# A down projection in seven products: ten pairs of K tiles in place of nine, set closer together, and later transpositions

## The chip, the cores and the metric

One program runs on one core of a Trainium2 chip. The metric is the device time of an execution in microseconds. Engines are named as the profile does: PE (TensorE), DVE (VectorE), ACT (ScalarE), POOL (GpSimd), SP (SyncE, which only issues DMAs here).

## The reference

One layer of a decoder trunk on 256 tokens of width 2048, all in fp32: two token mixers and their output projection, a gated feed-forward part, and a gated addition of a per-layer embedding.

```python
x = x + jnp.concatenate([ha, hb], axis=-1) @ w_out[i]
h = rms_norm(x, ffn_norm_g[i])
u = h @ w_up[i]                                   # 2048 -> 2 * 5632
a, g = jnp.split(u, 2, axis=-1)
a = causal_dwconv(a, conv_w[i], conv_b[i])        # width 3
x = x + (jax.nn.gelu(a, approximate=False) * g) @ w_down[i]      # 5632 -> 2048
gate = jax.nn.sigmoid(rms_norm(x, ple_norm_g[i]) @ w_ple_gate[i])
x = x + gate * (p[i].astype(x.dtype) @ w_ple_proj[i])
```

The change is in the product with `w_down` and in what follows it directly.

## The kernel before

Each fp32 product is made of three products in the narrower format fp32r: a matrix is split into `hi`, its rounding, and `lo`, the rest, and `hi*hi`, `hi*lo` and `lo*hi` are added in PSUM. Weights come as raw fp32 blocks of 128 rows by 1024 columns (512 KB) on SP's queue; ACT makes `hi` by a cast (line 836), DVE makes `lo` by a subtraction (line 837). Activations are split once, when they are made.

The work is a list of units (`Unit`), each with its loads (`load`), its split (`split`) and its matmuls (`fn`). `run_units` walks the list: ahead of a unit's matmuls it emits loads as long as raw buffers are free (3, and 2 more, `RAW2`, from the first unit of the down projection on) and splits up to 4 units ahead (7 in the down projection, `PARTS + PARTS2`). The framework's scheduler then sets the order of the instructions on each engine and its DMA queue; that order is fixed before the run, and each engine follows it, waiting on semaphores.

The down projection (`down`) runs in two halves of 1024 output columns, one after the other. Each half runs over 44 K tiles of 128, as 22 pairs, and in four PSUM banks it gathers the result by two halves of the tokens (`t`) and two of the columns (`n`); more banks hold what several of them share.

- An ordinary pair is two units of `eight`: for each K tile four products of 3 matmuls (lines 882 to 884) of 512 columns, so 24 matmuls a pair. A unit takes one raw block, one cast and one subtraction, each 1024 wide.
- A pair in `SEVEN` is taken as a 2x2 block matrix and multiplied by a scheme of seven block products in place of eight: 21 matmuls in four units. The first (`split1`) loads the kept left sums on SP's queue (line 913) and splits 512 columns of the first raw block, the second (`split2`) splits the second block; then `split3` and `split4` each make two sums of weights in place, by two DVE subtractions of 512 columns (lines 930 and 931, 940 and 941), and split the 1024 columns that come of it. A pair holds its two raw blocks until the third and the fourth split are done.

The left sums of these pairs are made in the up projection: `up_g` calls `left_sums` for each pair in `SEVEN` (lines 760 to 771), which makes four sums on DVE, splits them and writes them to DRAM through POOL's queue. In the down projection they are read back into two buffers in turn, so a load must wait until PE has done the seven-pair before last.

At the last pair in `SEVEN`, `sums_done` adds the shared banks to `xs` on DVE; after the last pair, `add_rest` adds the other four (line 995). The last stage, the gate, needs `xs` transposed (`transposes`, `transpose_x`, line 149): the first eight tiles hang on units of the second half, the last eight on the first units of the gate's first group, `g_`, whose eight units each use two tiles.

Of the kernel before, what the change touches and what calls it, by code (L numbers as in the profile page):

```python
# [33 lines left out]
RAW, PARTS = 3, 4  # L34
RAW2, PARTS2 = 2, 3

SEVEN = (2, 4, 6, 8, 10, 12, 14, 16, 18)
AHEAD_DMA, AHEAD_SPLIT = 3, 3
PAD = 16

# [5 lines left out]
def layer_kernel(  # L46
# [21 lines left out]
    def f32(ap):  # L68
        return ap.bitcast(F32)
# [63 lines left out]
    def split_T(dst, src, scale=None):  # L133

        hi, lo = dst[..., 0:256], dst[..., 256:512]
        if scale is None:
            act.copy(hi, src)
            dve.tensor_sub(lo, src, f32(hi))
        else:
            act.activation(hi, src, AF.Copy, scale=scale)  # L140
            dve.scalar_tensor_tensor(out=lo, in0=src, scalar=scale, in1=f32(hi),  # L141
                                     op0=ALU.mult, op1=ALU.subtract)

    def transpose_x(dst, k0, g):

        for k in (k0, k0 + 1):
            bk = bank("aux", f"xT{k}")
            for t in range(NT):
                pe.transpose(bk[:, t * P : (t + 1) * P], xs[:, t, k * P : (k + 1) * P], ident)
            split_T(dst[:, k, :], bk[:, 0:256], scale=g[:, k : k + 1])  # L150
# [91 lines left out]
    def token_group(w, korder, actT, c0, n, finish, tag="mm", prep=None, load=None):  # L242

        st = {}
        blocks = []
        kb = min(BLK // n, 2 * len(korder))
        starts = [(k0, kb) for k0 in korder[:: kb // 2]]
        if load is not None:
            starts = [(0, 1), (1, 1)] + starts[1:]
        for bi, (k0, kb) in enumerate(starts):  # L250
            def fn(hi, lo, bi=bi, k0=k0):
                if bi == 0:
                    st["b"] = [bank(tag, f"tg{t}") for t in range(NT)]
                for t in range(NT):
                    o = st["b"][t][:, :n]
                    for i in range(hi.shape[1]):
                        a = actT()[:, k0 + i, :]
                        ah, al = a[:, t * P : (t + 1) * P], a[:, 256 + t * P : 256 + (t + 1) * P]
                        first = bi == 0 and i == 0
                        last = bi == len(starts) - 1 and i == hi.shape[1] - 1  # L260
                        pe.matmul(o, ah, hi[:, i, :], start=first, stop=False)  # L261
                        pe.matmul(o, ah, lo[:, i, :], start=False, stop=False)  # L262
                        pe.matmul(o, al, hi[:, i, :], start=False, stop=last)  # L263
                    if bi == len(starts) - 1:
                        finish(t, st["b"][t])
            pair = k0 % 2 == 0
            blocks.append((wsrc(w, k0, kb, c0, n), fn, pair and prep and (lambda k0=k0: prep(k0)) or None,
                           pair and load and (lambda k0=k0: load(k0)) or None))
        return blocks
# [445 lines left out]
    with tc.tile_pool(name="ffn", bufs=1) as fp, tc.tile_pool(name="kept", bufs=1, space=bass.MemoryType.DRAM) as kp:  # L715
# [12 lines left out]

        sums = kp.tile([len(SEVEN), P, 1024], F32, name="sums")

# [29 lines left out]
        def left_sums(p_, u):  # L760

            (a11, a21), (a12, a22) = ((u[:, j, 0:P], u[:, j, P:S]) for j in range(2))
            f = sm.tile([P, 512], F32, tag="junk", name="Sf").rearrange("p (i c) -> p i c", i=4)
            dve.tensor_add(f[:, 0], a21, a22)
            dve.tensor_sub(f[:, 1], f[:, 0], a11)
            dve.tensor_sub(f[:, 2], a11, a21)
            dve.tensor_sub(f[:, 3], a12, f[:, 1])
            t = fp.tile([P, 4, 256], F32R, tag="pT", name="Sp")
            act.copy(t[:, :, 0:P], f)
            dve.tensor_sub(t[:, :, P:256], f, f32(t[:, :, 0:P]))  # L770
            pool.dma_start(out=sums[SEVEN.index(p_)], in_=f32(t).rearrange("p i c -> p (i c)"))

        def up_g(q):
            st = {}

            def f(jj, b):
# [5 lines left out]
                if j == 1:  # L782
                    dve.tensor_mul(u, u, gl.pop((q, pair)))
                    dst = uA[:, k : k + 2, :] if k < KD else uB[:, k - KD : k - KD + 2, :]
                    split_T(dst, u)
                    if k // 2 in SEVEN:
                        left_sums(k // 2, u)
# [51 lines left out]
        def units(blocks):  # L839
            return [Unit([b[0]], b[1], shift=b[4] if len(b) > 4 else 0) for b in blocks]  # L840
# [22 lines left out]
        def down(c0, X_tag, P_tag, sums_done, done, at):  # L863
# [4 lines left out]
            pairs = range(KF // 2)  # L868
            plain = [p_ for p_ in pairs if p_ not in SEVEN]
            total = {"P1": len(SEVEN), "P5": len(SEVEN), "P6": len(SEVEN), "P7": len(SEVEN)}  # L870
            for t in range(NT):
                for n in range(2):
                    total[t, n] = 2 * len(plain) + (len(SEVEN) if (t, n) != (1, 1) else 0)

# [90 lines left out]
        def get_x3T():  # L965
            if "t" not in x3T:
                x3T["t"] = new_aT("x3T")
            return x3T["t"]
# [30 lines left out]
        def transposes(*ks):  # L999
            return lambda *_: [transpose_x(get_x3T(), k0, g_ple) for k0 in ks]  # L1000
# [25 lines left out]
        def gate_done(c0, n, last):  # L1026
            def f(t, b):
                if "r" not in r3:
                    r3["r"] = rstd_of(ssq3, "ple")
                sg = fp.tile([P, 2, S], F32, tag="gl", name="sg", bufs=3).rearrange("p a b -> p (a b)")[:, :n]  # L1030
                w = n // 2 if last and t == NT - 1 else n
                for c in range(0, n, w):
                    sc = sg[:, c : c + w]
                    act.activation(sc, b[:, c : c + w], AF.Sigmoid, scale=r3["r"][:, t : t + 1])
                    dve.tensor_mul(sc, sc, pj[t][:, c : c + w])
                    dve.tensor_add(sc, sc, xs[:, t, c0 + c : c0 + c + w])
                    q = act if last and t == NT - 1 and c else nc.sync
                    q.dma_start(out=out[0, t * P : (t + 1) * P, c0 + c : c0 + c + w], in_=sc)
            return f

        def with_after(u, hook):
            fn = u.fn
            u.fn = lambda hi, lo: (fn(hi, lo), hook())
# [10 lines left out]
        for c0, n in ((0, 512), (512, 512), (1024, 512), (1536, 256), (1792, 256)):  # L1054
            g_ = units(token_group(w_ple_gate, all_k, get_x3T, c0, n, gate_done(c0, n, c0 == 1792)))
            p_ = units(token_group(w_ple_proj, [0], lambda: pT["t"], c0, n, proj_done, tag="aux"))
            if c0 == 0:
                for i in range(4):
                    with_after(g_[i], transposes(8 + 2 * i))
            at = len(g_) // 2  # L1060
            us += g_[:at] + p_ + g_[at:]
        run_units(us, first_late)
# [30 lines left out]
```

## Time and profile before

| | us |
|---|---|
| runs, median of 3 | 1280.36 (1279.6 to 1280.57) |
| the profiled execution | 1280.42 |
| its span, first to last instruction | 1278.7 |
| PE busy in it | 1269.0 |
| DVE busy in it | 851.3 |
| ACT busy in it | 681.8 |

The granted TensorE clock was 1.00 in the mean. The profile is of one execution. Its busy times are sums over instructions, taken over the whole kernel; the down projection runs from 938.5 to about 1169 us and has shares of its own, which the views by stretch show. A wait is put down to the work that ended last before it.

### The profile page before, as it was taken

What the parts mean: (1) busy time and instruction counts of PE and PEld (TensorE: products, weight loads), DVE (VectorE), ACT (ScalarE), POOL (GpSimd) and SP (SyncE); (2) the same over time, 40 slices, a digit from 0 to 9 for tenths busy, and PEclk for the clock granted to TensorE, in tenths of its full rate; (3) what the DMA queues carried; (4) which work ended last, traced back from release to release, by engine and by line L of the source; (5) the groups of instructions that cost most, each with busy time, mean ns of one, the idle gap of its engine ahead of it and who ended that gap; (6) DMA issues with size and microseconds to landing.
All of it is one profiled execution on the core that took longest, in us unless ns stands there. A gap on an engine that the chain in (4) does not pass through costs nothing.

```text
span 1278.7 us, 18356 instructions
## 1 busy us (share of the span) xinstructions
PE 1269.0 (99%) x7006; PEld 1112.0 (87%) x7006; DVE 851.3 (67%) x1173; ACT 681.8 (53%) x1011; POOL 23.6 (2%) x43
## 2 busy tenths in 40 slices
PE   9999999999999999999999999999999999999998
PEld 7899999988888888888888888888887788887888
DVE  6455566554555566776767676676778899898553
ACT  7655554434544455555555455555545556556442
POOL 2000000000000000000000000000000000000000
PEclk9999999999999999999999999999999999999999
DMA  8676755546555656676666766666767776777661
GB/s 249 172 188 186 209 172 147 153 134 180 170 187 180 188 180 197 185 210 202 198 198 204 209 191 207 206 207 190 213 220 245 259 281 221 253 243 238 198 192 46
DMA packets 124474, 252.87 MB, mean 198 GB/s; under 512 B 8377, under 2 KB 28193, under 8 KB 124385
## 3 DMA queue, kind: packets, MB, share of 16 engines
q1 hardware_dynamic: 122400, 246.51, 63.8%
q0 software_dynamic: 1600, 5.01, 1.1%
q8 instruction: 55, 0.90, 0.3%
q14 instruction: 34, 0.28, 0.1%
q10 hardware_dynamic: 385, 0.16, 0.0%
HBM read 244.84 MB, written 6.82 MB: 197 GB/s over the span
## 4 chain that ended last, share of the span: by engine, by line
PE 92%; DMA 3%; DVE 3%; ACT 1%; issue 0%; SPq 0%; DVEq 0%; ACTq 0%
PE wg L311 25%; PE wg L312 13%; PE tg L263 11%; PE tg L262 10%; PE tg L261 10%; DMA raw<-in_w_down_dram 2%; PE fg L287 2%; PE fg L289 2%; PE fg L288 2%; DMA raw<-in_w_in_dram 1%; DVE w L837 1%; PE dnP L884 1%; PE dnP L883 1%; PE dnP L882 1%; PE dn(0, 0)_9875 L884 1%; PE dn(0, 0)_9875 L882 1%
## 5 line engine op out<-in xcount | busy, mean ns | idle before, releaser
L311 PE MATMUL wg<-x2T,hi 128*128 128x512 f32 x1408 | 488.3, 392 | 0.0
L837 DVE TENSOR_TENSOR lo<-raw,hi 128x1024 fp32r<-128x1024 f32 (+1 forms) x268 | 320.3, 1203 | 177.2 <-ACT hi L836 176.3
L836 ACT CAST hi<-raw 128x1024 fp32r<-128x1024 f32 (+1 forms) x268 | 275.5, 1035 | 280.1 <-PE wg L311 177.4
L312 PE MATMUL wg<-x2T,lo 128*128 128x256 f32 x1408 | 393.5, 280 | 0.0
L311 PEld LDWEIGHTS wg<-x2T,hi 128*128 128x128 f32 x1408 | 264.1, 188 | 56.4
L233 DVE TENSOR_TENSOR lo<-raw,hi 128x1024 fp32r<-128x1024 f32 (+2 forms) x161 | 179.5, 1116 | 159.5 <-ACT hi L231 158.9
L312 PEld LDWEIGHTS wg<-x2T,lo 128*128 128x128 f32 x1408 | 267.3, 190 | 0.1
L231 ACT CAST hi<-raw 128x1024 fp32r<-128x1024 f32 (+2 forms) x161 | 154.6, 960 | 174.0 <-PE tg L263 100.4
L262 PE MATMUL tg<-lo,hT 128*128 128x512 f32 (+1 forms) x384 | 136.6, 356 | 0.5 <-DVE lo L233 0.5
L261 PE MATMUL tg<-hi,hT 128*128 128x512 f32 (+1 forms) x384 | 136.1, 358 | 0.0
L263 PE MATMUL tg<-hi,hT 128*128 128x512 f32 (+1 forms) x384 | 135.7, 355 | 0.0
L836 ACT CAST w<-raw 128x1024 fp32r<-128x1024 f32 x69 | 67.4, 988 | 57.9 <-DMA raw<-in_w_down_dram 22.1
L837 DVE TENSOR_TENSOR w<-raw,w 128x1024 fp32r<-128x1024 f32 x69 | 78.2, 1143 | 24.8 <-ACT w L836 24.4
L262 PEld LDWEIGHTS tg<-lo,hT 128*128 128x128 f32 x384 | 72.2, 188 | 8.2 <-DVE lo L233 1.0
L263 PEld LDWEIGHTS tg<-hi,hT 128*128 128x128 f32 x384 | 72.0, 188 | 7.7 <-DVE hT L141 0.3
L261 PEld LDWEIGHTS tg<-hi,hT 128*128 128x128 f32 x384 | 71.8, 188 | 7.1
L287 PE MATMUL fg<-hT,hi 128*128 128x256 f32 x256 | 74.3, 290 | 0.0
L289 PE MATMUL fg<-hT,lo 128*128 128x256 f32 x256 | 72.8, 284 | 0.0
L288 PE MATMUL fg<-hT,hi 128*128 128x256 f32 x256 | 72.4, 283 | 0.0
L261 PE MATMUL tg<-hi,catT 128*128 128x512 f32 x128 | 50.3, 393 | 0.0
L263 PE MATMUL tg<-hi,catT 128*128 128x512 f32 x128 | 50.0, 390 | 0.0
L262 PE MATMUL tg<-lo,catT 128*128 128x512 f32 x128 | 49.8, 389 | 0.0
(503 smaller groups left out, 1761.6 us busy)
## 6 DMA issues: line engine op xcount, KB each, us to landing
raw<-in_w_up_dram SPq DMA_DIRECT2D x176, 512.0 KB, 4.2
raw<-in_w_down_dram SPq DMA_DIRECT2D x88, 512.0 KB, 5.4
raw<-in_w_in_dram SPq DMA_DIRECT2D x79, 512.0 KB, 3.8
raw<-in_w_in_dram SPq DMA_DIRECT2D x48, 344.0 KB, 3.6
raw<-in_w_out_dram SPq DMA_DIRECT2D x32, 512.0 KB, 4.5
raw<-in_w_ple_gate_dram SPq DMA_DIRECT2D x32, 512.0 KB, 4.5
w<-sums SPq DMA_DIRECT2D x18, 512.0 KB, 5.1
sums<-Sp POOLq DMA_DIRECT2D x9, 512.0 KB, 4.8
```

The costliest lines, as they stand in the source:

```text
L231: act.copy(hi, raw[:, :w])
L233: dve.tensor_sub(lo, raw[:, :w], f32(hi))
L261: pe.matmul(o, ah, hi[:, i, :], start=first, stop=False)
L262: pe.matmul(o, ah, lo[:, i, :], start=False, stop=False)
L263: pe.matmul(o, al, hi[:, i, :], start=False, stop=last)
L287: pe.matmul(o, hi[:, i, cols], a[:, 0:256], start=first, stop=False)
L288: pe.matmul(o, hi[:, i, cols], a[:, 256:512], start=False, stop=False)
L289: pe.matmul(o, lo[:, i, cols], a[:, 0:256], start=False, stop=last)
L311: pe.matmul(o, hi[:, i, cols], a, start=first, stop=False)
L312: pe.matmul(o[:, 256:512], lo[:, i, cols], a[:, 0:256], start=False, stop=last)
L836: act.copy(hi, raw)
L837: dve.tensor_sub(lo, raw, f32(hi))
```

## The change

`SEVEN` gets ten pairs in place of nine. The first is pair 3 in place of 2 and the last 17 in place of 18; between them mostly two of three pairs are in it, where every second one was. The last four calls of `transposes` hang on the units 1 to 4 of the gate's first group in place of 0 to 3.

```diff
-SEVEN = (2, 4, 6, 8, 10, 12, 14, 16, 18)
+SEVEN = (3, 5, 6, 8, 9, 11, 12, 14, 15, 17)
...
             if c0 == 0:
                 for i in range(4):
-                    with_after(g_[i], transposes(8 + 2 * i))
+                    with_after(g_[i + 1], transposes(8 + 2 * i))
```

Everything that depends on `SEVEN` goes with it: the left sums made and kept in the up projection, their loads in both halves, and the counts of the products that end an accumulation.

## The prediction

> **What bounds the kernel now.** I read the page first, then the busy time of each engine in stretches cut at the borders of the down projection, then who waited for whom there, and last the single instructions of TensorE (PE) and VectorE (DVE).
>
> ```profile
> span 1278.7 us, 18356 instructions
> PE 1269.0 (99%) x7006; PEld 1112.0 (87%) x7006; DVE 851.3 (67%) x1173; ACT 681.8 (53%) x1011; POOL 23.6 (2%) x43
> PE 92%; DMA 3%; DVE 3%; ACT 1%; issue 0%; SPq 0%; DVEq 0%; ACTq 0%
> ...
> raw<-in_w_down_dram SPq DMA_DIRECT2D x88, 512.0 KB, 5.4
> ```
>
> PE is never long without work and carries 92% of the chain that ended last, so a matmul less is time less, as long as its operands are there. The averages hide the stage that changes. By stretch (pairs 3 to 18 of the first column half; the change of halves; most of the second half):
>
> ```profile
> core 0: us, PE busy (x) PEld busy (x) DVE busy (x) ACT busy (x) POOL busy (x), PEclk, DMA share, GB/s
> 953.00:1037.50 84.50, 82.97 (x362) 67.13 (x361) 73.22 (x82) 44.88 (x49) 0.00 (x0) 1.00 0.76 249
> 1037.50:1054.00 16.50, 16.50 (x74) 13.66 (x74) 15.86 (x16) 9.96 (x11) 0.00 (x0) 1.00 0.88 317
> 1054.00:1152.00 98.00, 98.00 (x434) 81.18 (x433) 87.67 (x98) 55.46 (x64) 0.00 (x0) 1.00 0.73 241
> ```
>
> Here DVE is busy 87 to 89% of the time, and PE has holes in the first half (82.97 of 84.50 us), none in the second. The waits (PE's from 938 to 1200 us, DVE's from 953 to 1040, SyncE's from 930 to 1180: total us, times, longest) name what PE lacked:
>
> ```profile
> PE dn(1, 0)_9017 L882 <- ACT hi L836: 0.8, 1, 0.8
> PE xT L149 <- DVE xs L995: 0.4, 2, 0.3
> PE dn(0, 0)_9009 L883 <- DVE lo L837: 0.4, 1, 0.4
> DVE raw L931 <- DMA raw<-in_w_down_dram: 4.6, 2, 2.8
> DVE w L837 <- ACT w L836: 3.8, 4, 1.8
> SPq L913 <- PE dnP L884: 30.2, 11, 4.6
> ```
>
> PE waits for split weights (`hi` of ScalarE, `lo` of DVE). DVE in turn waits for raw weights to land, and for ScalarE, whose cast reads the same raw weights. The last row is the load of the kept sums on SyncE's queue: it waits for PE to be done with an older pair, and the weight loads queued behind it wait too. So the down projection sits at the border between a bound by PE and a bound by the splitting, and the question is to which side the change moves it.
>
> **Part 1: matmuls removed.** The seventh part of a 24-matmul pair:
>
> ```profile
> 938.53 0.40 PE L882 MATMUL dn(0, 0)_9009<-hi,uA 128*128 128x512 f32 x1
> ...
> 942.89 0.60 PE L1015 MATMUL pTp<-ident,pr 128*128 128x128 f32 x4
> ...
> 1055.47 0.39 PE L882 MATMUL dn(0, 0)_9875<-hi,uA 128*128 128x512 f32 x1
> ...
> 1166.31 0.39 PE L882 MATMUL dn(0, 0)_9875<-w,uB 128*128 128x512 f32 x1
> ...
> 1168.80 0.40 PE L884 MATMUL dn(1, 1)_9887<-w,uB 128*128 128x512 f32 x1
> ```
>
> From 1166.31 to 1168.80 are 11 steps: a matmul follows the last after 0.2265 us (its own 0.39 us overlaps). A pair in eight products is 24 matmuls, 5.44 us; in seven, 21, 4.76 us. One pair more in each of two halves removes 6 matmuls: **-1.36 us**, all on PE's path.
>
> **Part 2: what DVE has to do for it.** One seven-pair and the eight-pair behind it:
>
> ```profile
> 987.72 0.68 DVE L837 TENSOR_TENSOR lo<-raw,hi 128x512 fp32r<-128x512 f32 x1
> 988.56 1.23 DVE L837 TENSOR_TENSOR lo<-raw,hi 128x1024 fp32r<-128x1024 f32 x1 [0.16 <-ACT hi L836]
> 989.70 0.69 DVE L930 TENSOR_TENSOR raw<-raw 128x512 f32<-128x512 f32 x1
> 990.42 0.69 DVE L931 TENSOR_TENSOR raw<-raw,raw 128x512 f32<-128x512 f32 x1
> 991.15 0.69 DVE L940 TENSOR_TENSOR raw<-raw,raw 128x512 f32<-128x512 f32 x1
> 991.87 0.69 DVE L941 TENSOR_TENSOR raw<-raw 128x512 f32<-128x512 f32 x1
> 992.48 1.22 DVE L837 TENSOR_TENSOR lo<-raw,hi 128x1024 fp32r<-128x1024 f32 x1
> 993.76 1.23 DVE L837 TENSOR_TENSOR w<-raw,w 128x1024 fp32r<-128x1024 f32 x1
> 995.29 2.36 DVE L837 TENSOR_TENSOR w<-raw,w 128x1024 fp32r<-128x1024 f32 x2 [0.30 <-ACT w L836]
> 997.57 0.68 DVE L837 TENSOR_TENSOR lo<-raw,hi 128x512 fp32r<-128x512 f32 x1
> ```
>
> The eight-pair takes 2.28 us from start to start (995.29 to 997.57). The stretch from 953.0 to 1037.5 holds 8 seven- and 8 eight-pairs in 73.22 us of DVE work, 9.15 us for one of each; so a seven-pair is 6.87 us. PE needs 4.76 us for it. Alternating, DVE has 9.15 us to do in PE's 10.20. Two of three, it has 2x6.87+2.28 = 16.0 us in PE's 2x4.76+5.44 = 14.96. In the dense stretch DVE is slower than PE even if it never waits; only its lead can pay for that.
>
> How far the lead goes I work out by DVE's time up to the fourth part of the last seven-pair, and test it on the kernel as it is:
>
> ```profile
> 949.14 0.42 DVE L138 TENSOR_TENSOR pT<-pTp,pT 128x256 fp32r<-128x256 f32 x1
> ...
> 950.80 2.48 DVE L837 TENSOR_TENSOR lo<-raw,hi 128x1024 fp32r<-128x1024 f32 x2
> ...
> 1036.16 1.23 DVE L837 TENSOR_TENSOR lo<-raw,hi 128x1024 fp32r<-128x1024 f32 x1
> ...
> 1060.35 0.68 DVE L995 TENSOR_TENSOR xs<-dn(1, 1)_9021,xs 128x512 f32<-128x512 f32 x1
> 1060.95 1.22 DVE L837 TENSOR_TENSOR w<-raw,w 128x1024 fp32r<-128x1024 f32 x1
> ```
>
> Test: pair 2 is split at 953.28 (950.80+2.48), pair 18 at 1037.39: 84.1 us, of which 73.2 work and 10.9 idle, 1.36 for each seven-pair. PE wants pair 18's fourth part after 423 matmuls, at 938.53+0.60 (the four transpositions)+95.8 = 1034.9. So the parts come 2.5 us late. What PE lost in that half: 501 matmuls are 113.5 us and 0.6, but the next half begins at 1055.47, 116.9 after 938.53: 2.8 us. Within 0.3 us the sum holds.
>
> First half after: the first seven-pair is pair 3, the last pair 17, with ten seven- and five eight-pairs from 949.56, when DVE is through with the rest of the up stage: 10x6.87+5x2.28 = 80.1 us. One correction: the small subtractions of a pair follow each other after 0.72 us (990.42, 991.15, 991.87), while an instruction behind a 512-wide one that it doesn't depend on follows after 0.60 (1060.35 to 1060.95). The scheduler sets each engine's order before the run, and in the changed program's order just 8 of 30 such neighbours are left in this half: 22x0.12 = 2.6 us at most. I take half, 1.3, as what is put between has waits of its own: 78.8 us. Idle: the pattern behind the measured 1.36 us is an eight-pair between two seven-pairs. The five raw buffers are refilled when DVE has read them, a load takes 5.4 us to land (median, the page), and the eight-pair covers 2.28 of it. That pattern is left at pairs 5, 8, 11, 14, 17: 5x1.36 = 6.8 us; between two seven-pairs in a row, 6.87 us of work cover the load. Done at 949.56+78.8+6.8 = 1035.2; PE wants it after 396 matmuls, at 938.53+0.60+89.7 = 1028.8. **PE waits 6.4 us**, in place of 2.8. Bounds: without idle time 0 (1028.4 against 1028.8), with 1.36 at all ten 13.2.
>
> Second half after: DVE begins pair 3 when the four residual adds of the half before are done, as now at 1060.95, 5.5 us after the half's first matmul (1055.47). PE wants the last part 89.7 us after that matmul, so there are 84.2 for the same 85.6: **1.4 us**, in place of none (bounds 0 and 8.2).
>
> Sum: -1.36 + (6.4+1.4) - 2.8 = **+3.6 us**. The profiled execution took 1280.42 us (1.7 outside its span), and the median is 1280.36: 1284.0 either way.
>
> [...]
>
> **Part 3: what comes along.** One pair's sums more in the up stage:
>
> ```profile
> L764 DVE TENSOR_TENSOR Sf<-u x9: 281/281/286, 541.8 to 896.8; 128x128 f32<-128x128 f32 x9
> L769 ACT CAST Sp<-Sf x9: 610/612/614, 545.8 to 900.8; 128x512 fp32r<-128x512 f32 x9
> L770 DVE TENSOR_TENSOR Sp<-Sf,Sp x9: 684/687/689, 547.1 to 902.1; 128x512 fp32r<-128x512 f32 x9
> 850.00:900.00 50.00, 50.00 (x290) 44.21 (x289) 37.01 (x60) 27.85 (x39) 0.53 (x1) 1.00 0.68 200
> ```
>
> Four small operations, a cast and a subtraction, 4x0.28+0.61+0.69 = 2.4 us once, beside PE that is busy 50.00 of 50 us while DVE has 13 us free: 0, and 2.4 if that cover were gone. Two more loads of sums, 1 MB in all, lie within what the stage moves (the 317 GB/s at the change of halves is above the 280 that two of three would ask for); but their buffers are two, so a load now waits for PE to end the seven-pair three pairs back, not four. Behind it on SyncE's queue stand the raw loads, for which DVE waits. This is in the idle time's upper bound, and the third rival.
>
> The later transpositions: each engine's order is the scheduler's, and only the last four transpositions move, behind the projection of `p`. The waits for `xT` (0.4 us) are at the first ones, whose banks the residual adds free, and stay. 0; at most 0.4 either way.
>
> **The rivals.**
> *Faster.* Loads under a pair of seven-pairs cover each other so well that nearly no idle time is left. For it: 6.87 us of work against a landing of 5.4. Against: DVE idled 10.9 us in the tested stretch, and 2.0 a half is the most that this case allows. PE then waits under 1.6 us in all; with no wait, 1280.36-1.36-2.8 = 1276.2.
>
> *Within the bound.* About 4.7 us idle a half: waits of 4.3 us in place of 2.8, and the six matmuls pay: 1280.5. From 2.0 to 6.2 us of idle a half the time stays between 1277.8 and 1282.9.
>
> *Much slower by the queue.* Sums that wait for PE hold back the weights at every seven-pair, 10x1.36 = 13.6 us idle a half: waits of 13.2 and 8.2 us, 1297.6. It decides once three pairs of PE work, some 15 us, no longer cover a load and the splitting behind it. For it: the 30.2 us of such waits; against: loads behind them still came in time through the whole second half.
>
> *Much slower by a serial VectorE.* Each instruction waits for the one before to end: 3x1.23+5x0.69 = 7.14 us a seven-pair, 2x1.23 = 2.46 an eight-pair, 83.7 us of work in place of 78.8; with 6.8 idle, waits of 11.3 and 6.3 us: 1293.8. Against: 73.22 us for 8 and 8 pairs, where that would be 76.8, so 1.14 us between starts is the rule of this stage. [...]
>
> What weighs against the faster case besides: in the order before, the three matmuls of a product are torn apart at 29 places, all in the first half, where PE was short of parts; in the new one at 85, in both halves and up to pair 20. That is an order, not a time, but it is what a scheduler does where it finds `lo` later than `hi`.
>
> **How the numbers follow.** Forecast (1282.9 to 1291) 0.50; faster 0.25; within 0.16; queue 0.05; serial VectorE 0.04. So faster by over 0.2% (2.56 us, about what a measurement of this kernel can tell from no change) 0.25, within 0.16, slower 0.59. The range from 1276.2 to 1291.0 leaves out those last two (0.09) and little else; the forecast's own is 1282.9 to 1291.
>
> **What would show it.** In the profile after: 996 down matmuls in place of 1002; PE busy clearly under its stretch in both halves, most behind pair 9, and the waits of PE for `hi` and `lo` grown from 1.2 us to some 5 (the view shows less than the starts do: 1.2 for 2.8); DVE over 90% busy between pairs 5 and 16. I am wrong if PE stays full there, which shows as DVE idle under 2 us a half; and the step on the transpositions is wrong if the waits for `xT` go.

## The result, and the profile after

| | before | after |
|---|---|---|
| median of 4 runs each, us | 1280.46 (1279.6 to 1282.89) | 1302.47 (1300.86 to 1304.17) |
| ratio | | 1.0181 [1.0168, 1.0194] |
| the profiled execution, us (span) | 1280.42 (1278.7) | 1304.17 (1302.5) |
| first half of the down projection, first matmul to first matmul of the next half | 938.53 to 1055.47: 116.9 | 938.39 to 1070.91: 132.5 |
| second half, first to last matmul | 1055.47 to 1168.80: 113.3 | 1070.91 to 1192.13: 121.2 |

The change makes the kernel 22 us slower, where 3.6 were forecast. Nearly all of it lies in the down projection: 15.6 us more in the first half, 7.9 in the second, 23.5 of the 23.8 by which the span grew.

The page of after, its first lines, the chain that ended last, and the weight loads:

```profile
span 1302.5 us, 18350 instructions
PE 1276.7 (98%) x7000; PEld 1111.2 (85%) x7000; DVE 860.4 (66%) x1190; ACT 685.5 (53%) x1016; POOL 24.1 (2%) x44
PE 86%; DMA 6%; DVE 5%; ACT 1%; issue 1%; SPq 0%; ACTq 0%; DVEq 0%
raw<-in_w_down_dram SPq DMA_DIRECT2D x88, 512.0 KB, 5.1
```

The six matmuls are gone (7000 for 7006), and six points of the chain have gone from PE to loads and DVE. By stretch, columns as in the prediction (dense stretch of the first half, change of halves, dense stretch of the second):

```profile
953.00:1046.00 93.00, 82.37 (x330) 62.50 (x329) 75.37 (x88) 43.67 (x48) 0.00 (x0) 0.96 0.62 209
1047.00:1074.00 27.00, 27.00 (x120) 22.32 (x120) 24.81 (x26) 16.27 (x19) 0.00 (x0) 1.00 0.92 306
1074.00:1166.00 92.00, 85.98 (x370) 68.42 (x369) 77.68 (x91) 46.90 (x55) 0.00 (x0) 1.00 0.63 213
```

PE has holes in both halves. But DVE, which was to be the bound, is busy 75.37 of 93.00 us, 81%, less than before. The rate of the loads fell too (209 GB/s, before 249). So no engine is full: they wait for one another. PE's waits from 938 to 1200 us, DVE's from 953 to 1046, SyncE's from 930 to 1180 (total us, times, longest):

```profile
PE dnP L882 <- ACT hi L836: 4.8, 4, 3.6
PE dn(1, 0)_9024 L882 <- ACT hi L836: 2.8, 4, 1.0
PE dn(0, 1)_9020 L882 <- DMA w<-sums: 2.0, 1, 2.0
DVE lo L837 <- ACT hi L836: 8.4, 7, 3.0
DVE w L837 <- ACT w L836: 6.4, 5, 3.0
DVE raw L931 <- DMA raw<-in_w_down_dram: 2.4, 3, 1.5
SPq L822 <- DVE w L837: 90.1, 37, 6.3
SPq L913 <- PE dnP L884: 28.7, 15, 4.8
```

DVE's waits behind a cast are 14.8 us. Before, in a stretch of like work (953 to 1040), they were 5.6: the 3.8 behind `w` that the prediction shows, and

```profile
DVE lo L837 <- ACT hi L836: 1.8, 4, 0.8
```

What such a wait is made of is seen instruction by instruction, in the order of time of DVE, then ScalarE, then SyncE's queue:

```profile
1000.44 0.69 DVE L930 TENSOR_TENSOR raw<-raw 128x512 f32<-128x512 f32 x1
1004.11 1.23 DVE L837 TENSOR_TENSOR w<-raw,w 128x1024 fp32r<-128x1024 f32 x1 [2.97 <-ACT w L836]
...
1017.47 0.69 DVE L837 TENSOR_TENSOR lo<-raw,hi 128x512 fp32r<-128x512 f32 x1 [2.46 <-ACT hi L836]
1020.42 0.68 DVE L941 TENSOR_TENSOR raw<-raw 128x512 f32<-128x512 f32 x1
1022.21 1.23 DVE L837 TENSOR_TENSOR w<-raw,w 128x1024 fp32r<-128x1024 f32 x1 [1.11 <-ACT w L836]
```

```profile
1003.02 1.05 ACT L836 CAST w<-raw 128x1024 fp32r<-128x1024 f32 x1 [4.14 <-DMA raw<-in_w_down_dram]
...
1016.82 0.62 ACT L836 CAST hi<-raw 128x512 fp32r<-128x512 f32 x1 [3.71 <-DMA raw<-in_w_down_dram]
1021.13 1.05 ACT L836 CAST w<-raw 128x1024 fp32r<-128x1024 f32 x1 [2.75 <-DVE raw L941]
```

```profile
996.10 4.06 SPq L822 DMA_DIRECT2D raw<-in_w_down_dram  x4
1000.35 0.57 SPq L913 DMA_DIRECT2D w<-sums  x1
1008.55 1.61 SPq L822 DMA_DIRECT2D raw<-in_w_down_dram  x2
```

The long waits (2.97, 2.46) are casts that wait for a load; the shorter one (1.11) is the chain inside a seven-pair: DVE ends a subtraction (L941), ScalarE casts the sum, DVE waits for the cast. The loads come in bursts. From 996.10 to 1000.35 four weight blocks and one of sums are issued on top of a load of sums at 995.73; the first of them lands only at 1003.0, after 6.9 us. Then no weight is issued until 1008.55, as all five raw blocks are held by pairs that wait for a load or a cast (the queue waits 7.6 us there for one split of VectorE). The load issued at 1009.83 lands at 1016.72, after 6.9 us too, and ends the second long wait.

### The profile page after: what moved, and what is told of

Its sections match the earlier page's. It is cut to its first block, busy times and chain, and to the rows that moved or that the text cites. A ratio compares the mean times of both kernels' runs of the same rounds, so it can differ in the third digit from the quotient of the medians.

```text
span 1302.5 us, 18350 instructions
## 1 busy us (share of the span) xinstructions
PE 1276.7 (98%) x7000; PEld 1111.2 (85%) x7000; DVE 860.4 (66%) x1190; ACT 685.5 (53%) x1016; POOL 24.1 (2%) x44
## 4 chain that ended last, share of the span: by engine, by line
PE 86%; DMA 6%; DVE 5%; ACT 1%; issue 1%; SPq 0%; ACTq 0%; DVEq 0%
PE wg L311 25%; PE wg L312 13%; PE tg L263 10%; PE tg L262 10%; PE tg L261 10%; DMA raw<-in_w_down_dram 4%; PE fg L287 2%; PE fg L289 2%; PE fg L288 2%; DVE lo L837 2%; DVE w L837 1%; DMA raw<-in_w_ple_gate_dram 1%; ACT hi L836 1%; DVE raw L940 1%; DMA raw<-in_w_in_dram 1%
## 5 line engine op out<-in xcount | busy, mean ns | idle before, releaser
L836 ACT CAST w<-raw 128x1024 fp32r<-128x1024 f32 (+1 forms) x70 | 68.8, 989 | 67.0 <-DMA raw<-in_w_down_dram 21.9
L837 DVE TENSOR_TENSOR w<-raw,w 128x1024 fp32r<-128x1024 f32 (+1 forms) x70 | 79.5, 1144 | 28.7 <-ACT w L836 28.2
```

Source lines behind the costliest of these rows:

```text
L836: act.copy(hi, raw)
L837: dve.tensor_sub(lo, raw, f32(hi))
```

## The experiments

The time of each run stands beside runs of the kernel before on the same chip; ratios are to those, with a 95% interval. The line numbers in a view are those of that run's own kernel, which its edit can shift. The scheduler makes a new order of every kernel, so a few us between two edits can be the order. Two theories were first: A, the spacing of the pairs; B, something that comes along (the transpositions, the number of pairs, the queue). Then, what makes the spacing dear: the amount of VectorE's work, the chain of cast and subtractions, or the loads.

**Transpositions, number, spacing.** Only the list, with the transpositions as before:

```diff
-                    with_after(g_[i + 1], transposes(8 + 2 * i))
+                    with_after(g_[i], transposes(8 + 2 * i))
```

> The ten new pairs, with the transpositions where they were. Theory A (the new pairs cost the 22 us, the transpositions nothing): 1301 to 1304 us, as the full change. Rival B (the later transpositions share the blame): 1285 to 1298 us.

1301.13 us, 1.0171 [1.0156, 1.0186]: the list has the loss; the transpositions have nothing that shows within the intervals. Ten pairs in the old spacing:

```diff
-SEVEN = (2, 4, 6, 8, 10, 12, 14, 16, 18)
+SEVEN = (2, 4, 6, 8, 10, 12, 14, 16, 18, 19)
```

> The kernel before with pair 19 as a tenth pair: one pair of neighbours in each half, else every second pair. Theory density (two of three asks more of VectorE, the five raw buffers and the loads than PE's time allows; a tenth pair as such does not): within 3 us of before, 1278 to 1283. Rival number (a tenth pair costs what was measured): 1295 us or more.

1282.29 us, 1.0026 [1.0013, 1.0039]. The first half was shorter than before (115.9 for 116.9 us), and the second lost nothing. What the run lost came behind them, 2.5 us of it one wait of PE for the residual add ahead of `xT`. Nine pairs in the new spacing, without 17:

```diff
-SEVEN = (3, 5, 6, 8, 9, 11, 12, 14, 15, 17)
+SEVEN = (3, 5, 6, 8, 9, 11, 12, 14, 15)
```

> Nine pairs, as before, but the first nine of the new list (without pair 17): as dense as the change, six matmuls more. Theory density: the stalls stay, 1296 us or more. Rival number: about 1280.

1306.78 us, 1.0213 [1.0198, 1.0228]. The spacing costs it, not the number.

**The queue** (the prediction's third rival). The changed kernel with the loads of the sums on GpSimd's queue:

```diff
-                    nc.sync.dma_start(out=f32(v).rearrange("p i c -> p (i c)"), in_=sums[SEVEN.index(p_)])
+                    pool.dma_start(out=f32(v).rearrange("p i c -> p (i c)"), in_=sums[SEVEN.index(p_)])
```

> The full change with the loads of the kept sums issued on GpSimd's queue in place of SyncE's, so that their wait for PE holds back no weights. Theory queue (the weights arrive late because they stand behind sums that wait for PE): most of the 22 us go, 1278 to 1288. Rival density (the raw buffers and VectorE are short in any case): 1296 or more. In between both have a part.

1304.27 us, 1.0192 [1.0175, 1.0209]. That no weights stand behind the sums any more changes nothing; this rival is out. PE's own waits for the sums fell from 4.0 us (2.0 in each half) to 0.9, and the time didn't follow. A third buffer for the sums wasn't tried.

**Buffers.** A part is the `hi` and `lo` of one unit. Six buffers of parts in place of seven (`PARTS2 = 2`), then the room of the seventh used as a sixth raw buffer:

> The full change with six in place of seven buffers for split weights, as a control for the next run. Theory buffers (the raw ring of five decides, not how far the splitting may run ahead): 1300 to 1306, as with seven. Rival lead (the change needs the seven parts): 1308 or more.

1298.18 us (two runs), 1.0145 [1.0121, 1.0168]: with fewer it is no slower.

> The full change with six raw buffers and six part buffers (to compare with five raw and six part buffers, 1298). Theory buffers (a load waits for the block five loads earlier): 1285 to 1292. Rivals VectorE and order: 1295 or more.

1295.92 us, 1.0128 [1.0113, 1.0143]: by these intervals a gain from the sixth raw block isn't shown. Two trials with a seventh raw block don't compute the reference, probably because blocks were overwritten while in use, so nothing is read from their times: after, 1327.0 us, and before, 1291.6.

> The full change with seven raw buffers in place of five in the down projection, and six part buffers. Theory buffers (a load can only start when VectorE is done with the block five loads earlier, and so lands too late): most of the 22 us go, 1279 to 1288. Rival VectorE (its work and its alternation with ScalarE set the pace): 1296 or more. In between: both.

> The kernel before with seven raw buffers and six part buffers. Theory buffers: its 2.8 us of waits in the first half go too, 1276 to 1279. Rival VectorE: 1279 to 1284.

**The order.** The weight loads chained in the order of the units (the scheduler had issued some of a later pair first), and then VectorE's splits and subtractions chained too:

```diff
-                    nc.sync.dma_start(out=raw[:, : kb * n].rearrange("p (k n) -> p k n", k=kb), in_=src)
+                    with (tc.issue_after(last["ld"]) if late and "ld" in last else ExitStack()):
+                        nc.sync.dma_start(out=raw[:, : kb * n].rearrange("p (k n) -> p k n", k=kb), in_=src)
+                    last["ld"] = traced()
```

> The full change with the weight loads of the down projection and the gate held in the order in which the units use them (the scheduler had moved, for example, the second block of pair 6 and a block of pair 7 ahead of the second block of pair 5). Theory order (the scheduler's exchanged loads make VectorE wait): 1285 to 1293. Rival VectorE (too much work in a dense stretch, whatever the order): 1298 to 1306.

1295.3 us, 1.0129 [1.0114, 1.0144], between the two ranges.

> The same, and VectorE's splits and subtractions of the down projection also held in the order of use (the scheduler had mixed those of neighbouring pairs). Theory order: 1281 to 1290, better than the loads alone. Rival VectorE: 1298 to 1306. If mixing was of use, slower than the loads alone.

1347.6 us, 1.0534 [1.0513, 1.0555]. VectorE's waits in it, from 945 to 1080 us:

```profile
DVE lo L839 <- ACT hi L838: 22.9, 14, 3.4
DVE w L839 <- ACT w L838: 16.4, 10, 2.9
```

This speaks for the scheduler's mixing of neighbouring pairs as what fills a good part of the waits of the chain, so that the changed kernel shows only the remainder. Loads in order and six raw buffers together:

> The changed kernel with the weight loads of the down projection in the order of the units and six raw buffers beside six buffers of parts. Alone the order gave 1295.3 and the buffers 1295.9, from 1302.5. Theory 'loads' (late weights, by their order and by buffers held, make VectorE idle): the two add up or more, 1282 to 1289. Theory 'chain': both touch the same small part, 1291 to 1296.

1298.13 us, 1.0141 [1.0125, 1.0156]: the two don't add up. Each of these kernels keeps over two thirds of the loss, so order and buffers are at most a part of the cause.

**The subtractions.** The changed kernel without lines 930, 931, 940 and 941:

> The full change without the four subtractions of weights in each seven-pair (the sums of weights are left out, so the result is not the reference's). VectorE has some 2.6 us less per pair and holds raw blocks shorter. Theory VectorE: all of the loss goes, 1277 to 1281. Theory buffers: half of it or less goes, 1288 to 1298, since casts and subtractions of halves still follow late loads.

1276.08 us, 0.9971 [0.9961, 0.9981]: all of the loss goes with them (their work, their links in the chain and the blocks that wait for them). On GpSimd in place of VectorE:

```diff
-                    dve.tensor_sub(half(ra, 0), half(ra, 1), half(ra, 0))
+                    pool.tensor_sub(half(ra, 0), half(ra, 1), half(ra, 0))
... the same for the other three
```

> The full change with the four subtractions of weights per seven-pair on GpSimd, idle in this stage, in place of VectorE. The work is all done, but 2.6 us per pair less of it by VectorE; the chain from a load to its parts gets no shorter. Theory VectorE's work: 1277 to 1284. Theory chain (it is the length of cast, subtraction, subtraction, cast, subtraction that keeps the blocks and the loads back): 1298 or more, longer still if GpSimd is slower per operation.

1329.8 us, 1.04 [1.038, 1.042]. Groups from 953 to 1046 us (GpSimd's first and last form, VectorE's splits):

```profile
L930 POOL TENSOR_TENSOR raw<-raw 128x512 f32<-128x512 f32 x10 | 16.6, 1665 | 99.1 <-DVE lo L837 95.9 <-DVE w L837 3.1
L940 POOL TENSOR_TENSOR raw<-raw,raw 128x512 f32<-128x512 f32 x9 | 18.8, 2091 | 6.4 <-DVE lo L837 4.9 <-DVE w L837 1.2
L837 DVE TENSOR_TENSOR lo<-raw,hi 128x1024 fp32r<-128x1024 f32 x21 | 34.1, 1637 | 17.6 <-ACT hi L836 17.4
```

A subtraction takes 1.67 to 2.09 us there (0.69 on VectorE), and VectorE's own split takes 1.64 in place of 1.22 beside it. So the chain is longer and VectorE is hardly relieved, and the run doesn't tell work from chain. The next two come closer. All work kept, the chain cut:

```diff
-                    dve.tensor_sub(half(ra, 0), half(ra, 1), half(ra, 0))
+                    dve.tensor_sub(half(lo, 0), half(ra, 1), half(ra, 0))
... the other three likewise into lo
```

> The changed kernel with all four weight subtractions of a seven-pair kept, at full width, on VectorE and at their places, but written into the lo buffer that the split overwrites next; the blocks keep their raw weights, so this kernel doesn't form the sums of weights. VectorE's work is that of the changed kernel; the chain load, subtraction, subtraction, cast, lo is two links shorter, and ScalarE's cast waits for the load alone. Theory 'chain' (the parts are late because cast and subtractions of one pair wait for each other in turn): most of the 22 us goes, 1276 to 1284 us. Theory 'work' (VectorE simply has too much to do where two of three pairs are in seven products, and its idle time follows from late loads): it stays within 5 us of the changed kernel, 1296 to 1303.

1293.97 us, 1.0109 [1.0092, 1.0126], between the two ranges. And the chain kept, its subtractions 64 columns wide:

```diff
-                    dve.tensor_sub(half(ra, 0), half(ra, 1), half(ra, 0))
+                    dve.tensor_sub(ra[:, 0 : 64], ra[:, 512 : 576], ra[:, 0 : 64])
... the other three likewise
```

> The changed kernel with the four weight subtractions of a seven-pair at their places and in their order, but 64 columns wide in place of 512; the sums of weights are formed for these columns alone. All waits of the chain stay, with links of some 0.2 us in place of 0.69; the work on VectorE falls by some 4x0.5 us a seven-pair, to 4.9 us, 59 us a half in place of 78.8. Theory 'work': as without the subtractions, 1276 to 1278. Theory 'chain': the links are four times shorter but the order of waits stays, so a part of the loss stays, 1280 to 1288; where it comes out at 1276, the length of the links matters and not that there are waits.

1278.43 us, 0.9992 [0.9983, 1.0002], just above the range of 'work'. From 953 us to about the last subtraction of the half, in the kernel with the chain cut and in the one with it narrow:

```profile
953.00:1040.00 87.00, 79.79 (x330) 61.31 (x328) 73.14 (x88) 44.51 (x50) 0.00 (x0) 0.98 0.66 224
```

```profile
953.00:1028.00 75.00, 74.16 (x327) 61.07 (x327) 60.33 (x91) 45.21 (x51) 0.00 (x0) 1.00 0.74 256
```

Both leave VectorE idle about 14 us in the first half (87.00-73.14 and 75.00-60.33; the changed kernel 93.00-75.37 = 17.6). With 60 us of work in it PE is hardly touched; with 73 to 75 it isn't to be hidden. Cutting the chain is worth 8.5 us, cutting the work as well as the length of the links 24. Last, loads of 64 KB in place of 512, with the chain and without:

```diff
... the raw buffers as five fixed tiles
+                    if whole and again:
+                        n, src = 128, src[:, :, 0:128]
...
```

> The changed kernel with weight loads of the down projection an eighth as wide (128 of 1024 columns, 64 KB in place of 512); the other columns keep what the buffer held, so the product is made with other weights. Casts, subtractions and matmuls, their order of dependence and the holding of buffers stay. Theory 'loads': with loads that land early VectorE's idle time goes from some 20 us in the first half to under 7 and the kernel takes 1277 to 1286 us. Theory 'chain': the waits between cast and subtractions stay, 1290 to 1302. Theory 'work': VectorE's 78 us of work have to fit anyway; by the prediction's sum without idle time that costs nothing, so what stays above 1280 with no idle is work.

1316.71 us, 1.0293 [1.0277, 1.0309].

> Both: the four subtractions written aside (as in e17, 1294.0 us) and the loads an eighth as wide; neither the sums nor the right weights are formed. What is left against the changed kernel is VectorE's work alone, at its full amount. Prediction's sum with idle time 0: 1276.2, so 1276 to 1280 if loads and chain explain all the loss; if work by itself is more than the sum had, 1284 to 1294. Theory 'chain': this is at least 8 us faster than e21; theory 'loads': within 3 us of it.

1287.8 us, 1.0066 [1.0049, 1.0083] (in this expectation e17 is the run with the chain cut, e21 the one with short loads alone). In both runs the loads land after 1.9 us (median), and with the chain the kernel gets no faster but 14 us slower. The stretch of the run with the chain, then what its VectorE waited for from 945 to 1055 us and its loads from 930 to 1180:

```profile
953.00:1046.00 93.00, 79.15 (x309) 58.64 (x308) 78.02 (x90) 45.00 (x50) 0.00 (x0) 0.95 0.21 66
```

```profile
DVE raw L951 <- DMA raw<-in_w_down_dram: 8.1, 8, 2.0
DVE lo L848 <- ACT hi L847: 8.0, 6, 2.9
SPq L833 <- DVE lo L848: 101.0, 43, 7.6
```

(L951 is line 940 of the changed kernel, L847 and L848 are 836 and 837.) It waits as before, with the DMA engines busy 21% of the time: the loads are late because they are issued late, when a split on VectorE gives a block free (the last row), not because they take long. That the time rose is not explained; the scheduler had another order here. The raw buffers are five fixed tiles in these two kernels, which may add to it. With the chain cut too the kernel is 29 us faster than with it, where with the long loads it was 8.5. The run with both, from the time where the prediction starts its sum to the end of the split behind the half's last subtraction:

```profile
949.56:1035.03 85.47, 82.17 (x356) 65.89 (x354) 77.71 (x92) 49.99 (x55) 0.00 (x0) 1.00 0.27 89
```

VectorE is idle 7.8 us here, near the 6.8 of the prediction, and the first half (938.61 to 1058.83, 120.2 us) loses 6.8 us, near its 6.4. So with the idle time about as small as was forecast, the loss is about as small too; as the scheduler's order is another one here, this is a hint and not a proof. The run is still 9 us slower than the kernel before, in the range that was given for work that costs more by itself than the sum had. But its VectorE is idle 14 us again from the first to the last subtraction of the second half, which loses 4.7 us (117.5 for 112.8) where 1.4 were forecast, so the price of the work alone can't be read from it.

**The kernel before with its loads in order** (the edit of the changed kernel's run above):

> The kernel before (nine pairs, every second one) with the weight loads of the down projection in the order of the units. Its first half loses 2.8 us to waits for parts. Theory 'loads': the loss shrinks to under 1, 1278 to 1279.5. Theory 'chain': no change, within 0.1% of 1280. If the order of the scheduler was there for a reason that I don't see, it is slower.

1278.2 us, 0.9991 [0.9981, 1.0000]. Its stretch, to be read beside the prediction's first, and its wait for a load (4.6 us before; L933 is line 931 there):

```profile
953.00:1037.50 84.50, 84.50 (x374) 70.02 (x373) 76.22 (x84) 47.28 (x52) 0.00 (x0) 1.00 0.76 260
```

```profile
DVE raw L933 <- DMA raw<-in_w_down_dram: 0.5, 1, 0.5
```

PE is full, and of the 2.8 us that the first half lost it has nearly all (114.1 for 116.9 us). It has the lowest median of all kernels that compute the reference, 1.1 us below the runs of the kernel before beside it (1279.31); by the interval the gain lies between 0.2% and nothing.

## Why the prediction was wrong

Right were the direction, the six matmuls (996 in the down projection), the extra left sums (PE 50.00 of 50 us from 850 to 900, as before), and the transpositions (by the run with the list alone, within the intervals). VectorE's work was right. The sum had 78.8 us of it and 6.8 idle from 949.56 us to the fourth part of the last seven-pair; the part came at 1047.93, and up to there VectorE was busy 78.18 us and idle 20.2:

```profile
949.56:1047.93 98.37, 87.59 (x351) 66.53 (x350) 78.18 (x91) 47.18 (x52) 0.00 (x0) 0.97 0.61 207
```

The frame of the sum was right as well: VectorE's time up to the fourth part of the last seven-pair says what PE loses. These are the last splits of the two halves:

```profile
1044.83 0.69 DVE L941 TENSOR_TENSOR raw<-raw 128x512 f32<-128x512 f32 x1
1045.44 1.22 DVE L837 TENSOR_TENSOR w<-raw,w 128x1024 fp32r<-128x1024 f32 x1
1046.71 2.36 DVE L837 TENSOR_TENSOR lo<-raw,hi 128x1024 fp32r<-128x1024 f32 x2
...
1165.29 0.69 DVE L941 TENSOR_TENSOR raw<-raw 128x512 f32<-128x512 f32 x1
1167.15 2.36 DVE L837 TENSOR_TENSOR lo<-raw,hi 128x1024 fp32r<-128x1024 f32 x2 [1.17 <-ACT hi L836]
```

The first half's is done at 1046.71+1.22 = 1047.9, where PE wanted it at 1028.8: 19.1 us late, and the half is 132.5-113.4 = 19.1 us longer than its matmuls. The second's is done at 1168.4, wanted at 1070.91+89.7 = 1160.6: 7.8 late, 8.4 measured. By these, -1.36+19.1+7.8-2.8 = +22.7, against 23.8 of the span.

The step that failed is one term: **VectorE's idle time, 6.8 us a half.** It came out at 17.6 in the first half between the first subtraction (952.8) and the last (1045.5), and 3 us more ahead of it, and at 14.3 in the second. The reason given for the small value was that only five places keep an eight-pair between two seven-pairs, and that 6.87 us of work between two seven-pairs in a row cover a load's 5.4. Three things were wrong in it. The cover was counted as work, but the work of a seven-pair is itself a chain of casts and subtractions that waits, and it holds two of the five raw blocks to its third and fourth split. The 5.4 us is a median: the four loads that were issued in a burst from 996.10 on took 6.9. (The loads as such were no slower than before: over the first half the median landing was 5.5 us before and 5.3 after. What differs is when they could be issued.) And the idle time isn't set by the neighbour: 11.3 us for nine pairs in the first half before, 17.6 and 14.3 for ten after, 14 in the first half with the chain cut or narrow. At 1.36 for each of the ten, which the prediction had as its upper bound, it would have been 1297.6 us.

Not all of the idle time starts at a cast or a weight load. One of the three waits of about 3 us in the first half starts at PE:

```profile
973.70 0.79 PE L882 MATMUL dn(0, 1)_9020<-w 128*128 128x512 f32 x1 [2.01 <-DMA w<-sums]
977.83 0.62 ACT L836 CAST hi<-raw 128x512 fp32r<-128x512 f32 x1 [4.30 <-PE dnP L884]
978.48 0.69 DVE L837 TENSOR_TENSOR lo<-raw,hi 128x512 fp32r<-128x512 f32 x1 [2.96 <-ACT hi L836]
```

PE waits 2.0 us for a load of sums and starts its next matmuls 0.43 us apart in place of 0.2265 (last section), ScalarE waits for PE to be done with a buffer of parts, and VectorE waits for the cast. What the half would have taken without this, no run shows; with the sums on GpSimd's queue, where PE waits less for them, the time was no better.

The 1297.6 us stood as the queue's rival, which came nearest in price, with the wrong cause: with the sums off SyncE's queue the loss stayed. The serial VectorE (1293.8) was not it either: it asked for 83.7 us of work where 78.18 were measured, and for 2.46 us for two 1024-wide splits in a row, which still took 2.36 (1046.71).

What weighed for a small loss, "idle time covered by work", is what the dense list takes away. In the kernel before, VectorE had 9.15 us to do for every 10.20 of PE, and most of its 11 us of idle time went into that spare time. In the dense one the work alone, by the prediction 16.0 us for PE's 14.96, takes all the time that PE gives, so what a cast or a load is late goes to PE. The narrow subtractions show it from the other side: about the same idle time, less work, hardly a loss. How the 24 us divide between the length of the links and the amount of the work, and how much of each is the scheduler's order, stays open: the runs that change one of them change the order as well, and the short loads with the chain, at 1316.7, fit none of the theories.

The signs that the prediction named were half right: PE's waits for `hi` and `lo` did grow, to over 10 us, but DVE over 90% busy was wrong in the direction. It fell to 81%.

## What to carry to other kernels

When an engine that feeds the bottleneck is brought near its limit, its idle time has to be added at least at the full measured rate for each unit that has a chain in it, and not only where the old pattern is repeated: here 1.36 us a unit before became 17.6 and 14.3 us for ten, and what had covered it was the spare time that the change uses up. A median landing time, here 5.4 us, doesn't say what loads take that are issued in a burst when buffers come free together, here 6.9. Before packing such units closer, look at what keeps the feeding engine waiting: here putting the loads in order took the old spacing's waits away, which was worth 0.2% at most.

## What the runs showed of the hardware

After two of its pauses in the first half PE ran at about half its rate for six and seven matmuls. The rows around the longer pause, and the stretch around it with a granted clock of 0.83:

```profile
1013.49 0.39 PE L882 MATMUL dn(0, 1)_9020<-w,uB 128*128 128x512 f32 x1
1017.49 0.50 PE L882 MATMUL dnP<-hi,uB 128*128 128x512 f32 x1 [3.61 <-ACT hi L836]
...
1018.54 0.63 PE L883 MATMUL dn(0, 1)_9020<-w,uB 128*128 128x512 f32 x1
1018.97 0.63 PE L884 MATMUL dn(0, 1)_9020<-w,uB 128*128 128x512 f32 x1
```

```profile
1012.00:1022.00 10.00, 6.39 (x22) 4.79 (x21) 6.64 (x9) 3.49 (x4) 0.00 (x0) 0.83 0.70 232
```

After 4.0 us without a start, matmuls follow each other after 0.43 us in place of 0.2265, from the third start on. The same came after a pause of 2.4 us at 971.30, which had one of 1.4 us just ahead of it (granted clock 0.79 from 970 to 978), but not after one of 2.3 us at 1149.89 (1.00 from 1149 to 1156). How long a pause has to be for it, no run shows. 13 matmuls of the first half ran so, 2.6 us that the prediction hadn't priced. They don't come on top of the sum, as the half ended when VectorE's last split let it (19.1 and 19.1 us late); but the first six of them stand ahead of one of VectorE's own waits, as the rows in the section above show.

The other surprise is that VectorE's fp32 splits were slower in the run where GpSimd subtracted fp32 tensors beside it (1.64 us in place of 1.22, above). Whether GpSimd was slowed too isn't shown, as no run has its subtractions alone; at 1.67 to 2.09 us in place of VectorE's 0.69, moving them there was worse than keeping them (1329.8 us, the changed kernel 1302.47).
